# A hybrid attention layer on one core: gates in halves, mixed tiles split earlier, residual tiles loaded in pairs, weight sums in mid-pair

## The chip, the cores and the metric

The kernel runs on one core of a Trainium2 chip. The metric is device time in microseconds (us) of one execution, as the median of the runs shown. The engines that matter are TensorE (PE in the profile, with PEld for its weight loads), VectorE (DVE), ScalarE (ACT), GpSimd (POOL) and SyncE (SP). In this kernel SP issues all DMA transposes and the stores, and POOL issues the loads of weights and of the residual. Each engine works through its own list of instructions in order; an instruction that waits holds all that stand behind it on that engine.

## What is computed

One layer over 1024 tokens of width 1024, with two groups of 8 heads that read the same normalised input, group A with full attention and group B with attention to a neighbourhood on a 16 x 64 grid. Cut to what matters:

```python
h = _rmsnorm(x, norm_gain[l])
proj = h @ w_in[l]                                   # 1024 x 3328
q_a, k_a, v_a, g_a, q_b, k_b, v_b, g_b = jnp.split(proj, split_at, axis=-1)
q_a, k_a = rope(_rmsnorm(q_a, q_norm_a[l])), rope(_rmsnorm(k_a, k_norm_a[l]))
o_a = _gqa_blocked(q_a, k_a, v_a) * jax.nn.silu(g_a)             # softmax over all keys
o_b = _neighbourhood_attn(q_b, k_b, v_b, na_rpb[l]) * jax.nn.silu(g_b)
mixed = jnp.concatenate([o_a, o_b], axis=-1)
x = x + mixed @ w_out[l]
return _rmsnorm(x, final_norm_gain)
```

`rope` stands for the reference's rotation by cosine and sine tables.

## The kernel before

**Precision.** Every matrix product is made from f16 halves: an operand is scaled, rounded to a high half, and the rest is its low half. A product is three matmuls, high x high, high x low and low x high. "Splitting" a tile means making both halves.

**Tokens.** The 1024 tokens are 8 units u of 128. Projections work on pairs of units (`up`, two units), each pair in one bank of PSUM with 2 x 24 matmuls of 128x256, so 48 matmuls a pair and 24 a chain. The pool `ps_p` of PSUM has two such banks; in the profile a bank is named by the pair that took it, `pj`, `kb`, `po`, or `wt` where a weight sum took it first.

**Weights.** The projections come in 17 groups g of 256 columns: 0 to 2 are k, v and q of group A, 3 to 8 q, k, v of group B, 9 and 10 the gates of B, 11 and 12 the gates of A, 13 to 16 the four blocks of w_out. A group's weights are loaded as f32 into one of two buffers `raw` (1 MB, POOL's queue). `prep_a` squares and sums them on ScalarE into `whl` (L287), `prep_b` adds the sum over the partitions with one tiny matmul into a projection bank (the "weight sum", L299), takes it out on VectorE (L300) and raises it to a power on POOL (L301); `prep_c` makes the high half on ScalarE (L306, twice), `prep_d` the low half on VectorE (L313, twice), and then group g+2 is loaded. The bank of the sum is the one that a later pair will use (list `ahead`), so the sum must wait until that bank's former values were taken out, and that pair until L300 has read the sum.

**Stages.** Phase 1 (to about 101 us) normalises x, transposes it and projects groups 0 to 2. Phase 2 (to about 360 us) runs 64 units of full attention (one head and one token unit each), each a step: QK on TensorE, softmax on VectorE and ScalarE, a DMA transpose of the probabilities, and P x V four steps later. Between them, groups 3 to 8 fill TensorE. Phase 3 (to about 573 us) does the same with 64 units of neighbourhood attention, P x V five steps later, filled with the gates 9 to 12 and then with the output projection of token units 0 to 4. The tail does the output projection of units 5 to 7. A step of phase 3 is QK of one unit (L675, L676), 18 matmuls of filling, and P x V of a former unit (L705 to L707). I count steps through both phases: full attention has steps 1 to 64, neighbourhood unit i is step 65 + i.

**Order.** `Flow.at(delay, pos, ...)` puts a piece of work at one of four places of a later step, "pre" (ahead of QK), "mid" (after QK), "post" (ahead of the filling) and "end". TensorE gets its instructions exactly in the order of the program. The order on the other engines is set by a scheduler, within the dependences, when the kernel is built.

**Mixed rows.** When a token unit's attention is gated, `os_a` (ScalarE's squares L731, VectorE L732 and L733, POOL L734), `os_b` (high half L739 on ScalarE, low half L743 on VectorE) and `os_c` (two DMA transposes, L748: the high half into mA, the low half into mB) split its mixed row for the output projection. The two halves live in a buffer `mhl` that units u and u+2 share, so the squares of u+2 wait for both transposes of u. In the kernel before, units 0 to 3 are split by delays after the last gates of A (`SPLIT_DELAY`), units 4 to 6 in fixed units (`SPLIT_AT`).

**Output.** `out_gen` makes 48 matmuls for two (unit, group) jobs, then VectorE adds them to the residual x2 (L779). x is loaded once more for that: x2 of units 0 and 1 into a `raw` buffer early, of units 2 and 3 together with w_out's third block into the old place of hT (`alloc_x2`, L759 and L762), of 4 and 5 after the last weights, of 6 and 7 after units 0 and 1 are stored. In the softmax of phase 3, L683 on VectorE finds the row's maximum mx, L685 on POOL scales it, L686 and L687 on ScalarE take the exponentials, L692 on VectorE makes the low half, and L694 on SP transposes.

Of the kernel before, what the change touches and what calls it, by code (L numbers as in the profile page):

```python
# [16 lines left out]
P = 128  # L17
# [11 lines left out]
SPLIT_AT = (39, 55, 56)  # L29
SPLIT_DELAY = (1, 2, 1, 3)  # L30
# [58 lines left out]
def kernel(ctx: ExitStack, tc: tile.TileContext, x: bass.AP, w: bass.AP, wo: bass.AP,  # L89
# [65 lines left out]
    def load_w(g):  # L155
        if g == 15:
            t = x2["a"] = wraw.tile([P, 2, 1024], F32, tag="raw", name="x2a")
            for u in range(2):
                x2[u] = t[:, u]
                load_x2(u)  # L160
            return
# [146 lines left out]
    def prep_d(g):  # L308
# [7 lines left out]
        if g == 15:  # L316
            load_x2(4)
            load_x2(5)
# [18 lines left out]

    def prep(g):
        if g == 2:
            at(5, "pre", prep_a, g)  # L340
            at(5, "end", prep_b, g)
            at(6, "pre", prep_c, g)
            at(6, "post", prep_d, g)
            at(7, "pre", load_w, g + 2)
            return
# [23 lines left out]
    def chunks(ops, n):  # L369
        for i in range(0, len(ops), n):  # L370
            for o in ops[i:i + n]:
                pe.matmul(*o[0], **o[1])  # L372
            yield

    def proj_pair(g, up, lhs, evac):
# [9 lines left out]
        for i in range(2):  # L385
            ops = [((pt[:, i], lhs(a, k, 2 * up + i), b[:, k]), dict(start=n == 0, stop=n == 23))
                   for n, (k, a, b) in enumerate(seq)]
            yield from chunks(ops, 6)
        evac(pt)
# [123 lines left out]
    def kb_gen(hh, pr, R):  # L513
# [10 lines left out]
        yield from chunks(ops, 3)  # L524
        if R == 0:
            khs[0] = slot("stg", [P, 1024], F16)
        kt = khs[0]
        cs = slice(R * 512, (R + 1) * 512)
        pp = 2 * hh + pr
        at(1, "pre", lambda: act.activation(kt[:, cs], pt, AF.Copy, scale=2.0 ** -14))  # L530
        at(1, "mid", lambda: dve.scalar_tensor_tensor(klo[:, pp, cs], pt, 2.0 ** -14, kt[:, cs],
                                                      op0=OP.mult, op1=OP.subtract))
        if R == 1:
            def cp():
                for e in range(2):
                    for half in range(2):
                        sp.dma_start(khh[half * D:(half + 1) * D, 2 * pp + e], kt[e * D:(e + 1) * D])
            at(1, "post", cp)
# [255 lines left out]
    def fin_b(u):  # L794
# [8 lines left out]
        if u < 2:  # L803
            load_x2(u + 6)
# [236 lines left out]
```

## Time and profile before

| what | value |
|---|---|
| runs (us) | 618.15, 621.88, 621.28 |
| median (us) | 621.28 |
| the profiled execution's own time (us) | 615.87 |
| its span, from the first to the last instruction (us) | 614.1 |
| mean granted clock of TensorE | 0.966 |
| TensorE busy (us, share of the span) | 530.4, 86% |
| VectorE, ScalarE, POOL busy (us) | 435.5, 394.9, 152.6 |

Every duration and wait below comes from that one profiled execution, which is 5.41 us shorter than the median of the runs. A line of a profile names the source line, the engine, the operation, what it writes and reads, and its time; "idle before, releaser" is how long the engine stood still ahead of it and what ended that. The granted clock is the share of full speed at which TensorE was allowed to work. Where the lines of the changed kernel are shown, line numbers are its own and lie some lines lower or higher than those of the kernel before.

### The profile page before, as it was taken

What the parts mean: (1) busy time and instruction counts of PE and PEld (TensorE: products, weight loads), DVE (VectorE), ACT (ScalarE), POOL (GpSimd) and SP (SyncE); (2) the same over time, 40 slices, a digit from 0 to 9 for tenths busy, and PEclk for the clock granted to TensorE, in tenths of its full rate; (3) what the DMA queues carried; (4) which work ended last, traced back from release to release, by engine and by line L of the source; (5) the groups of instructions that cost most, each with busy time, mean ns of one, the idle gap of its engine ahead of it and who ended that gap; (6) DMA issues with size and microseconds to landing.
All of it is one profiled execution on the core that took longest, in us unless ns stands there. A gap on an engine that the chain in (4) does not pass through costs nothing.

```text
span 614.1 us, 13949 instructions
## 1 busy us (share of the span) xinstructions
PE 530.4 (86%) x5541; PEld 405.8 (66%) x5541; DVE 435.5 (71%) x922; ACT 394.9 (64%) x647; POOL 152.6 (25%) x214
## 2 busy tenths in 40 slices
PE   3487989799998999888798989999999767999794
PEld 1375878577774555456676777777777545787683
DVE  4688767977978888777888746565778835877332
ACT  5552645768688688667687646776788957864210
POOL 2386688500000000000000002231324411433100
PEclk9987999999999999999998999999999978999898
DMA  8989543799999999999999974373749979749522
GB/s 231 224 162 234 100 114 95 141 209 197 212 191 186 196 189 196 202 204 172 202 172 183 184 211 119 55 143 65 134 81 151 209 126 177 143 78 199 120 61 69
DMA packets 245971, 97.26 MB, mean 158 GB/s; under 512 B 236561, under 2 KB 237201, under 8 KB 243986
## 3 DMA queue, kind: packets, MB, share of 16 engines
q1 hardware_dynamic: 242306, 75.66, 68.4%
q0 software_dynamic: 3312, 19.92, 11.3%
q10 hardware_dynamic: 288, 0.79, 0.5%
q8 instruction: 43, 0.70, 0.5%
q14 instruction: 22, 0.18, 0.1%
HBM read 31.33 MB, written 4.19 MB: 58 GB/s over the span
## 4 chain that ended last, share of the span: by engine, by line
PE 46%; DMA 23%; DVE 11%; issue 7%; ACT 7%; POOL 4%; SPq 1%; DVEq 0%; POOLq 0%; ACTq 0%
PE pj L372 12%; PE wt L372 10%; DMA ar<-p 9%; PE po L372 7%; DMA mB<-mhl 4%; DMA ar<-ar 3%; PE kb L372 3%; PE s L594 3%; PE s L596 2%; PE sb L676 2%; ACT p L605 2%; ACT p L606 2%; POOL nt L417 2%; DMA pt<-ar 1%; DMA hT<-xhl 1%
## 5 line engine op out<-in xcount | busy, mean ns | idle before, releaser
L372 PEld LDWEIGHTS <-hT 128*128 128x128 f16 x2112 | 207.0, 100 | 76.0 <-issue 19.9
L372 PE MATMUL pj<-whl,hT 128*128 128x256 f16 x1536 | 183.3, 276 | 3.7 <-DMA hT<-xhl 3.7
L372 PE MATMUL wt<-whl,hT 128*128 128x256 f16 x576 | 74.4, 287 | 21.8 <-DVE wss L300 8.9
L603 DVE CUSTOM_DVE_ANT_0 p<-s,sm 128x1024 f32<-128x1024 f32 x64 | 81.9, 1279 | 13.8 <-PE s L596 8.5
L605 ACT ACTIVATE p<-s,nm,sm 128x1024 f16<-128x1024 f32 x43 | 51.8, 1205 | 48.9 <-DMA ar<-p 26.7
L606 ACT ACTIVATE p<-s,nm,sm 128x1024 f32<-128x1024 f32 x64 | 76.9, 1202 | 0.0
L372 PE MATMUL po<-whl,mA 128*128 128x256 f16 x416 | 72.1, 279 | 0.0
L686 ACT ACTIVATE rq<-ar,mx,sm 128x384 f32<-128x384 f32 (+1 forms) x64 | 43.2, 676 | 35.4 <-POOL mx L685 32.9
L611 DVE TENSOR_TENSOR p<-p,p 128x1024 f16<-128x1024 f32 x43 | 52.5, 1221 | 18.4 <-ACT p L606 18.3
L685 POOL TENSOR_SCALAR mx<-mx,sm 128x1 f32<-128x1 f32 x64 | 31.9, 498 | 111.5 <-DVE mx L683 96.9
L372 PE MATMUL po<-whl,mB 128*128 128x256 f16 x208 | 57.9, 278 | 0.0
L301 POOL TENSOR_TENSOR sm<-wss,mh 128x1 f32<-128x1 f32 x17 | 13.4, 789 | 178.2 <-DVE wss L300 177.7
L372 PEld LDWEIGHTS <-mA 128*128 128x128 f16 x512 | 49.3, 100 | 12.3 <-issue 3.9
L594 PE MATMUL s<-kTa,rq 128*128 128x512 f16 x128 | 38.5, 382 | 14.4 <-ACT p L606 14.4
L692 DVE TENSOR_TENSOR ar<-rq,ar 128x384 f16<-128x384 f32 (+1 forms) x64 | 34.2, 536 | 18.0 <-ACT ar L687 17.7
L687 ACT ACTIVATE ar<-ar,mx,sm 128x384 f16<-128x384 f32 (+1 forms) x64 | 42.8, 674 | 1.2
L313 DVE SCALAR_TENSOR_TENSOR whl<-raw,sm,whl 128x1024 f16<-128x1024 f32 (+1 forms) x31 | 41.5, 1348 | 1.3 <-ACT whl L306 1.3
L625 PE MATMUL pv<-va,ar 128*128 128x64 f16 x384 | 38.7, 193 | 3.3 <-DMA ar<-p 2.0
L625 PEld LDWEIGHTS <-ar 128*128 128x128 f16 x384 | 34.5, 98 | 7.2 <-DMA ar<-p 3.3
L627 PE MATMUL pv<-va,ar 128*128 128x64 f16 x384 | 38.7, 193 | 0.0
L626 PE MATMUL pv<-va,ar 128*128 128x64 f16 x384 | 38.7, 193 | 0.0
L306 ACT ACTIVATE whl<-raw,sm 128x1024 f16<-128x1024 f32 x32 | 35.0, 1141 | 3.4 <-POOL sm L301 3.2
(200 smaller groups left out, 1071.7 us busy)
## 6 DMA issues: line engine op xcount, KB each, us to landing
raw<-in_w_dram POOLq DMA_DIRECT2D x11, 1024.0 KB, 6.2
x<-in_x_dram SPq DMA_DIRECT2D x7, 512.0 KB, 6.5
raw<-in_wo_dram POOLq DMA_DIRECT2D x3, 1024.0 KB, 6.1
khh<-ar SPq DMA_DIRECT2D x16, 128.0 KB, 2.9
x2a<-in_x_dram POOLq DMA_DIRECT2D x4, 512.0 KB, 7.6
x2b<-in_x_dram POOLq DMA_DIRECT2D x4, 512.0 KB, 7.9
out_dram<-x2b SPq DMA_DIRECT2D x8, 256.0 KB, 3.6
out_dram<-x2a SPq DMA_DIRECT2D x7, 256.0 KB, 3.1
```

Of the source, the lines that this page charges most:

```text
L313: dve.scalar_tensor_tensor(wp[g][1][:, s], raw[g][:, s], col(S_ + g), wp[g][0][:, s], op0=OP.mult, op1=OP.subtract)
L372: pe.matmul(*o[0], **o[1])
L594: pe.matmul(s[:, c * 512:(c + 1) * 512], q, kTa[:, 4 * c:4 * c + 4, hh], start=True, stop=False)
L603: dve.tensor_tensor_reduce(out=p32, in0=s, in1=col(SHA).to_broadcast([P, 1024]), scale=col(NSA), scalar=3e38, op0=OP.add, op1=OP.min, accu ...
L605: act.activation(hl[:, 0], s, AF.Exp, bias=nm, scale=col(SCA))
L606: act.activation(p32, s, AF.Exp, bias=nm, scale=col(SCA), accum_out=sums[hh, u][:, h:h + 1])
L611: dve.tensor_tensor(hl[:, 1], p32, hl[:, 0], op=OP.subtract)
L625: pe.matmul(o, pt[:, kt], va[:, kt, hh, 0], start=kt == 0, stop=False)
L626: pe.matmul(o, pt[:, kt], va[:, kt, hh, 1], start=False, stop=False)
L627: pe.matmul(o, pt[:, 8 + kt], va[:, kt, hh, 0], start=False, stop=kt == 7)
L686: act.activation(p32, t, AF.Exp, bias=mx, scale=col(SCB + hh), accum_out=sums["b", u][:, h:h + 1])
L687: act.activation(hl[:, 0], t, AF.Exp, bias=mx, scale=col(SCB + hh))
```

## The change

It has four parts.

1. The gates of A are no longer made group by group (group 11 for all four pairs, then group 12) but by halves of the tokens: group 11 for pairs 0 and 1, group 12 for pairs 0 and 1, then both for pairs 2 and 3. The mixed rows of token units 0 to 3 are now split in the fixed units 26, 27, 29 and 31 (plus the five of the skew, which makes 32 to 37), through the same hook as those of 4 to 6. The delays of the weights' preparation stand in the table `PREP`.
2. A weight sum is no longer issued ahead of a step's filling, but at the end of a chain, so in the middle of a pair (`sums_now`, called by `chunks`); it still goes into the bank of the next pair. The high halves, the low halves and the load of g+2 follow one, one and two steps later. What takes a pair's values out is set going in the step of the pair's last matmul and no longer in the call after it.
3. x2 of units 0 and 1 is loaded when the last gates are done, of units 2 and 3 after the first additions to units 0 and 1 (`more_x2`; a copy from x2 of unit 1 on POOL holds the load back until then), of units 4 and 5 after the low halves of group 15, of 6 and 7 after those of group 16. w_out's third block is loaded into the ordinary `raw` buffer.
4. The scaling of mx in the softmax of phase 3 (L685, 64 instructions of 128x1) moves from POOL to VectorE. The words for the change do not name this.

The core of the diff:

```diff
-SPLIT_AT = (39, 55, 56)
-SPLIT_DELAY = (1, 2, 1, 3)
+SPLIT_AT = (26, 27, 29, 31, 39, 55, 56)
+PREP = {2: 4, 3: 0, 4: 2, 12: 0, 13: 0}
...
-        if g == 15:
-            load_x2(4)
-            load_x2(5)
+        if g > 14:
+            t = wraw.tile([P, 2, 1024], F32, tag="raw", name=f"x2{g}")
+            for i in range(2):
+                x2[2 * g - 26 + i] = t[:, i]
+                load_x2(2 * g - 26 + i)
...
     def prep(g):
...
-        d = 0 if g < 4 else 2 if g == 4 else 1
+        d = PREP.get(g, 1)
         at(d + 1, "pre", prep_a, g)
-        at(d + 2, "post", prep_b, g)
-        at(d + 3, "pre", prep_c, g)
-        at(d + 3, "post", prep_d, g)
-        if g + 2 < 17:
-            at(d + 4, "pre", load_w, g + 2)
+        at(d + 2, "mid", pend.append, g)
+
+    def sums_now():
+
+        while pend:
+            g = pend.pop(0)
+            prep_b(g)
+            at(1, "pre", prep_c, g)
+            at(1, "post", prep_d, g)
+            if g + 2 < 17:
+                at(2, "pre", load_w, g + 2)
...
-    def chunks(ops, n):
+    def chunks(ops, n, then=None):
         for i in range(0, len(ops), n):
             for o in ops[i:i + n]:
                 pe.matmul(*o[0], **o[1])
+            if i + n >= len(ops):
+                (then or sums_now)()
...
-        pool.tensor_scalar(mx, mx, col(NSB + hh), LN_P, op0=OP.mult, op1=OP.add)
+        dve.tensor_scalar(mx, mx, col(NSB + hh), LN_P, op0=OP.mult, op1=OP.add)
...
     def alloc_x2():
-        c = one.tile([P, 2, 2, 1024], F32, tag="hT1", name="x2b")
-        raw[15] = c[:, 0].rearrange("p a (b c) -> p (a b) c", c=GC)
-        for u in range(2, NU):
-            x2[u] = x2["a"][:, u - 6] if u > 5 else c[:, int(u < 4), u % 2]
-
+        c = one.tile([P, 4, 1024], F32, tag="hT1", name="x2b")
+        for u in range(4):
+            x2[u] = c[:, u]
+        load_x2(0)
+        load_x2(1)
+
+    def more_x2():
         for u in (2, 3):
-            pool.tensor_copy(x2[u][:, :1], rws[3][:, 3:4])
+            pool.tensor_copy(x2[u][:, :1], x2[1][:, :1])
             load_x2(u)
-        pool.dma_start(raw[15], wo[2])
...
+        def then():
+            at(1, "mid", add)
+            if jobs[-1] == (1, 13):
+                at(1, "post", more_x2)
...
-    fl.add(*group(11, [g_gen(11, up, mixA, slice(0, GC), False) for up in UP]))
-    fl.add(*group(12, [g_gen(12, up, mixA, slice(GC, 512), False) for up in UP]))
+    ga = [[g_gen(GA + i, up, mixA, slice(i * GC, i * GC + GC), False) for up in UP] for i in range(2)]
+    fl.add(*group(11, ga[0][:2]), *ga[1][:2], *ga[0][2:], *group(12, ga[1][2:]))
```

On TensorE the first projection step of the output (units 0 and 1, group 13) begins at step 106 and that of units 2 and 3 at step 109, in both kernels. The weight sum of group 13 stands at step 98 before and at step 105 now, that of group 14 at step 109 before and at step 110 now; the first matmuls with these weights stand at steps 106 and 112. Between a sum and the first matmul with its weights lay 54 matmuls or more for groups 13 and 14, and lie 24 for groups 13 to 16 now, beside QK and P x V.

**SP, the middle of phase 3.** L694 (L692 now) are the softmax transposes, one a step; L748 are the two transposes of a mixed row, of units 0 (mhl_6077), 1 (mhl_6130), 2 (mhl_6224) and 3 (mhl_6304). Before:

```order
132 L694 DMA_TRANSPOSE ar<-ar 128x6x128 x27
133 L748 DMA_TRANSPOSE mA_1058<-mhl_6077 128x8x128
134 L748 DMA_TRANSPOSE mB_4725<-mhl_6077 128x8x128
135 L694 DMA_TRANSPOSE ar<-ar 128x6x128
136 L748 DMA_TRANSPOSE mA_1058<-mhl_6130 128x8x128
137 L748 DMA_TRANSPOSE mB_4725<-mhl_6130 128x8x128
138 L694 DMA_TRANSPOSE ar<-ar 128x6x128 x4
139 L748 DMA_TRANSPOSE mA_1059<-mhl_6224 128x8x128
140 L748 DMA_TRANSPOSE mB_4726<-mhl_6224 128x8x128
141 L694 DMA_TRANSPOSE ar<-ar 128x6x128
142 L748 DMA_TRANSPOSE mA_1059<-mhl_6304 128x8x128
143 L748 DMA_TRANSPOSE mB_4726<-mhl_6304 128x8x128
```

Now, with units 0 (mhl_5986), 1 (mhl_6038), 2 (mhl_6130) and 3 (mhl_6227); eight softmax transposes stand ahead of the first row in both:

```order
132 L692 DMA_TRANSPOSE ar<-ar 128x6x128 x21
133 L748 DMA_TRANSPOSE mA_1072<-mhl_5986 128x8x128
134 L692 DMA_TRANSPOSE ar<-ar 128x6x128
135 L748 DMA_TRANSPOSE mB_4725<-mhl_5986 128x8x128
136 L692 DMA_TRANSPOSE ar<-ar 128x6x128 x2
137 L748 DMA_TRANSPOSE mA_1072<-mhl_6038 128x8x128
138 L748 DMA_TRANSPOSE mB_4725<-mhl_6038 128x8x128
139 L692 DMA_TRANSPOSE ar<-ar 128x6x128
140 L748 DMA_TRANSPOSE mA_1073<-mhl_6130 128x8x128
141 L748 DMA_TRANSPOSE mB_4726<-mhl_6130 128x8x128
142 L692 DMA_TRANSPOSE ar<-ar 128x6x128 x5
143 L748 DMA_TRANSPOSE mA_1073<-mhl_6227 128x8x128
```

Unit 0's first transpose stood behind 35 softmax transposes and now stands behind 29; unit 2's stood behind 40 and now stands behind 32, unit 3's behind 41 and now behind 38.

**ScalarE, at the first output projections.** L731 are the squares of units 4 (mhl_6576, now mhl_6564) and 5 (mhl_7253, now mhl_7257). L306 (L300 now) makes the high halves of the next weights, of group 14 before (whl_6473) and of group 13 now (whl_6210). Before:

```order
361 L287 ACTIVATE whl_6734,wss_6735<-x2b 128x2048
362 L686 ACTIVATE rq,sumb_6346<-ar,mx_2_6431,sm 128x384
363 L731 ACTIVATE mhl_6576,os_6575<-mA_1060 128x512
364 L686 ACTIVATE rq,sumb_6346<-ar,mx_3_6478,sm 128x384
365 L306 ACTIVATE whl_6473<-raw_5702,sm 128x1024 x2
366 L687 ACTIVATE ar<-ar,mx_2_6431,sm 128x384
```

Now:

```order
352 L685 ACTIVATE ar<-ar,mx_7_6300,sm 128x384
353 L731 ACTIVATE mhl_6564,os_6563<-mA_1074 128x512
354 L684 ACTIVATE rq,sumb_6339<-ar,mx_0_6340,sm 128x384
355 L731 ACTIVATE mhl_7257,os_7256<-mA_1074 128x512
356 L300 ACTIVATE whl_6210<-raw_5304,sm 128x1024 x2
357 L685 ACTIVATE ar<-ar,mx_0_6340,sm 128x384
358 L562 ACTIVATE ar<-pj_3_6309,sm 128x512
```

The first squares of unit 5 moved ahead of a weight group's high halves, which were group 14's and are group 13's now.

**POOL and VectorE, at the additions to x.** On POOL, L759 before loaded w_out's third block and L762 x2 of units 2 and 3; L685 is the scaling of mx, L734 belongs to a split. Before:

```order
146 L685 TENSOR_SCALAR mx_1_6387<-mx_1_6387,sm 128x1
147 L759 DMA x2b<-in_wo_dram 128x2048
148 L734 TENSOR_TENSOR os_6303<-os_6303,mh 128x1
149 L685 TENSOR_SCALAR mx_2_6431<-mx_2_6431,sm 128x1
150 L757 COPY x2b<-os_6303 128x1 x2
151 L762 DMA x2b<-in_x_dram 128x1x1024 x2
```

Now, where L763 loads x2 (units 0 and 1 first, then 2 and 3), L159 w_out's third block, and L759 is the copy that holds the second load back:

```order
101 L295 TENSOR_TENSOR sm<-wss_6211,mh 128x1
102 L715 TENSOR_TENSOR mB_4727<-mB_4727,ar 128x256
103 L763 DMA x2b<-in_x_dram 128x1x1024 x2
104 L159 DMA raw_6425<-in_wo_dram 128x2048
105 L759 COPY x2b<-x2b 128x1 x2
106 L763 DMA x2b<-in_x_dram 128x1x1024 x2
```

On VectorE now, L772 is the addition of units 2 and 3, L307 the low halves of group 14 (whl_6469), L681 and L683 belong to a softmax:

```order
739 L690 TENSOR_TENSOR ar<-rq,ar 128x384
740 L740 RECIPROCAL os_6563<-os_6563 128x1
741 L772 SCALAR_TENSOR_TENSOR x2b<-po_13_6524,rw_13_6525,x2b 128x256 x2
742 L307 SCALAR_TENSOR_TENSOR whl_6469<-raw_5702,sm,whl_6469 128x1024
743 L681 ISA ar,mx_7_6658<-sb_4734,bias_4800 128x384
744 L681 ISA mx_7_6658 128x1
745 L307 SCALAR_TENSOR_TENSOR whl_6469<-raw_5702,sm,whl_6469 128x1024
746 L683 TENSOR_SCALAR mx_7_6658<-mx_7_6658,sm 128x1
```

Before, the low halves of group 14 (L313) stood ahead of that addition (L779):

```order
683 L313 SCALAR_TENSOR_TENSOR whl_6473<-raw_5702,sm,whl_6473 128x1024 x2
684 L683 ISA ar,mx_6_6619<-sb_4733,bias_4800 128x384
685 L683 ISA mx_6_6619 128x1
686 L692 TENSOR_TENSOR ar<-rq,ar 128x384 x2
687 L732 TENSOR_TENSOR os_6575<-os_6575 128x1
688 L779 SCALAR_TENSOR_TENSOR x2b<-wt_6522,rw_13_6532,x2b 128x256 x2
```

The load of x2 for units 2 and 3 moved behind w_out's third block and behind the additions of units 0 and 1, and the addition of units 2 and 3 moved ahead of group 14's low halves.

More of the change, by code (lines that the diff above doesn't have):

```diff
@@ L569, in mul @@
                 dve.scalar_tensor_tensor(m, th, col(G2 + g - GB), m, op0=OP.mult, op1=OP.mult)
+                ready.add(("a", up, cols.start))
             at(1, "mid", mul)
[L571 to L575 removed]
             if g == GA + 1 and up == 3:
@@ L726, in os_a @@
     def os_a(u):
+        assert all({("b", u, c), ("a", u // 2, c * GC)} <= ready for c in range(2))
         t = rws[u] = tn(f"os{u}", 4, "os")
```

79 lines of the change are left out of this document (31 added, 48 removed).

## The prediction

> **What bounds the kernel now.** I read the page of the profile first, then TensorE's waits, then the chain of waits, then the stretches of the span in which the chain leaves TensorE, and last the timelines of the queues there. The page:
>
> ```profile
> span 614.1 us, 13949 instructions
> PE 530.4 (86%) x5541; PEld 405.8 (66%) x5541; DVE 435.5 (71%) x922; ACT 394.9 (64%) x647; POOL 152.6 (25%) x214
> ```
>
> TensorE is busy for 530.4 of 614.1 us, so what can be won without less work are its 84 us of idle time and the time it runs at a lower clock. The change removes no matmul. Its worth is therefore a list of TensorE's waits that go and waits that come. TensorE's waits (us in total, how often, the longest):
>
> ```profile
> PE s L594 <- ACT p L606: 14.4, 12, 1.9
> PE wt L372 <- DVE wss L300: 13.5, 10, 2.5
> PE wt L372 <- DMA mB<-mhl: 7.0, 1, 7.0
> PE sb L705 <- DMA ar<-ar: 5.5, 2, 4.4
> PE pvb L705 <- DMA ar<-ar: 2.6, 1, 2.6
> PE wt L299 <- DVE x2a L779: 0.9, 1, 0.9
> PE wt L299 <- DVE ar L568: 0.6, 1, 0.6
> PE wt L299 <- DVE mB L565: 0.5, 1, 0.5
> ```
>
> Rows 2 and 6 to 8 are the weight sums (L299, and L300 behind it): 13.5 + 0.9 + 0.6 + 0.5 = 15.5 us. Row 3 is the out-projection waiting for the low half of unit 2's mixed rows. Rows 4 and 5 are neighbourhood attention waiting for softmax transposes. The chain (start, duration, what) shows where these lie:
>
> ```profile
> 442.66 2.07 PE pj L372 x18
> 445.42 2.07 PE pj L372 x18
> ...
> 470.04 5.32 DMA mB<-mhl
> ...
> 483.41 12.75 DMA mB<-mhl
> ...
> 532.50 0.75 DVE x2a L779 x2
> ...
> 573.04 23.99 PE po L372 x208
> ```
>
> An undisturbed step of phase 3 takes 445.42 - 442.66 = 2.76 us, a matmul 23.99 / 208 = 0.115. From 483 to 496 us the program waits for one transpose of 12.75 us, where that of unit 0 had taken 5.32. Three timelines (SP, POOL, ACT) show what lay beside it and what stood behind it:
>
> ```profile
> 483.41 4.20 SPq L748 DMA_TRANSPOSE mB<-mhl  x1
> 481.83 0.64 POOL L759 DMA_DIRECT2D x2b<-in_wo_dram  x1
> 484.12 1.13 POOL L762 DMA_DIRECT2D x2b<-in_x_dram  x2 [0.17 <-POOL x2b L757]
> 496.18 0.63 ACT L731 ACTIVATE mhl<-mA 128x512 bf16<-128x512 f32 x1 [5.53 <-DMA mB<-mhl]
> 497.50 2.17 ACT L306 ACTIVATE whl<-raw,sm 128x1024 f16<-128x1024 f32 x2
> ```
>
> One 1 MB and two 512 KB loads were issued within 3.4 us around it, and ScalarE stood 5.53 us at the squares of unit 4 (they share unit 2's buffer), with the scaling of the next weights behind. The stretches after such waits (length, busy us of PE, PEld, DVE, ACT, POOL, then clock, DMA share, GB/s):
>
> ```profile
> 492.00:495.00 3.00, 0.00 (x0) 0.00 (x0) 0.00 (x0) 0.00 (x0) 0.00 (x0) 0.50 1.39 146
> 495.00:498.00 3.00, 1.71 (x9) 1.21 (x10) 0.00 (x0) 1.82 (x5) 0.00 (x0) 0.50 1.25 225
> 498.00:501.00 3.00, 3.00 (x23) 1.94 (x22) 1.54 (x6) 3.00 (x5) 0.99 (x2) 0.59 0.37 74
> 510.00:513.00 3.00, 2.64 (x19) 1.58 (x20) 1.83 (x6) 2.97 (x6) 0.92 (x2) 0.62 1.54 186
> 513.00:516.00 3.00, 3.00 (x28) 2.20 (x27) 1.58 (x5) 1.25 (x3) 0.33 (x1) 0.81 0.86 174
> 121.00:124.00 3.00, 2.69 (x14) 1.96 (x14) 2.66 (x13) 3.00 (x7) 1.47 (x1) 0.60 1.03 194
> 124.00:127.00 3.00, 3.00 (x40) 2.30 (x38) 2.32 (x2) 1.94 (x2) 0.00 (x0) 0.83 1.10 126
> 92.00:95.00 3.00, 3.00 (x30) 2.70 (x28) 1.65 (x5) 1.29 (x2) 3.00 (x5) 1.00 0.27 50
> ```
>
> After the 7.0 and 2.6 us waits, and after one of 2.48 us that ends at 121, the granted clock is 0.50 to 0.62 for a slice; after one of 2.04 us that ends at 91 it stays at 1.00. TensorE's busy time times what the clock lacks is 1.7 x 0.50 + 3 x 0.41 = 2.1 us after the first, 2.64 x 0.38 + 3 x 0.19 = 1.6 after the second, 2.69 x 0.40 + 3 x 0.17 = 1.6 after the third. I price a wait of over 2.4 us at its length and 1.8 us more.
>
> **Removed.** (1) Unit 2's transpose: with the gates of A in halves unit 2 is transposed behind 32 softmax transposes instead of 40, eight steps or 22 us earlier for the same place of use, and the two x tiles and wo's third block leave the burst at 482. Its cover is these 22 us, more than the worst 12.75. 7.0 + 2.1 = 9.1 us. (2) The transpose wait at 510 (2.6 + 1.6 = 4.2) and the two at 567 and 573 (5.5 + 1.8 = 7.3), if the softmax transposes no longer queue behind split transposes and x loads: 11.5. (3) and (4) The sums. Single waits of theirs (the last number; the third kind comes four times, the first and the last shown):
>
> ```profile
> 91.31 0.49 PE L372 MATMUL wt<-whl,hT 128*128 128x256 f16 x3 [2.04 <-DVE wss L300]
> 121.31 0.56 PE L372 MATMUL wt<-whl,hT 128*128 128x256 f16 x3 [2.48 <-DVE wss L300]
> 151.25 0.49 PE L372 MATMUL wt<-whl,hT 128*128 128x256 f16 x3 [1.45 <-DVE wss L300]
> 284.88 0.49 PE L372 MATMUL wt<-whl,hT 128*128 128x256 f16 x3 [1.45 <-DVE wss L300]
> ```
>
> (3) Phase 3 has what is left of 13.5 without these: 13.5 - 2.0 - 2.5 - 4 x 1.45 = 3.2 us, and the three evacuation waits of 0.9, 0.6 and 0.5: 5.2. With (1) and (2) phase 3 loses 9.1 + 11.5 + 5.2 = 25.8 us.
> (4) Phase 2 has the 2.48 us with its clock, 4.1 us, and four of 1.45: 5.8, together 9.9. These four do not turn into time one for one: in phase 2 the next bound is close by, as the 14.4 us in twelve waits for ScalarE's L606 show, and this stretch of 15 us:
>
> ```profile
> 300.00:315.00 15.00, 13.10 (x177) 10.47 (x176) 11.90 (x20) 10.71 (x15) 0.00 (x0) 1.00 1.01 180
> ```
>
> The DMA engines' share is 1.01 there, and TensorE idles for 1.9 of 15 us with no sum near. I take the early 4.1 and a fifth of the 5.8: 5.3 us, with 0 and 9.9 as ends.
>
> **Added.** The sum now comes 24 matmuls ahead of the first use of its weights (groups 13 to 16), where those of 13 and 14 had 54. What must happen in between, in the sums of before (group 13):
>
> ```profile
> 456.99 0.15 DVE L300 TENSOR_SCALAR wss<-wt 128x1 f32<-128x1 f32 x1
> 458.67 2.17 ACT L306 ACTIVATE whl<-raw,sm 128x1024 f16<-128x1024 f32 x2
> 459.88 2.48 DVE L313 SCALAR_TENSOR_TENSOR whl<-raw,sm,whl 128x1024 f16<-128x1024 f32 x2
> ```
>
> From L300 to the end of the first low half (459.88 + 1.24) are 4.1 us, and the sum itself lies some 0.5 before: 4.6. 24 matmuls are 24 x 0.115 = 2.8 us, and the QK and PV of a step 2.76 - 2.07 = 0.7: 3.5 or, with two such, 4.2. So a bare wait of 0.4 to 1.1 us, four times, and at two places more. The first sum that moves so is group 2's, in phase 1: no QK or PV beside it, 4.6 - 2.8 = 1.8 us of wait in the place of the 2.04 that ended at 91, 1.8 more if the clock falls. Ends -2.0 (hidden) and +2.3 (as the 2.48 us wait, with its clock): I take +1, the clock being nearer to falling there than not.
> S1, group 13. The low half stands behind ScalarE's hi, and this now stands behind the squares of unit 5 (L731), which wait until both transposes of unit 3 have landed. The row for such a place is the 5.53 us wait above; a transpose like unit 0's (5.32) frees it sooner than that of 12.75. I take 3, about the middle between 0.4 and 5.53, 1.4 for the evacuation that the sum itself now meets (the 0.9 and 0.5 rows together), and the clock's 1.8: 6.2. Ends 2 and 13 (the 12.75 us transpose again).
> S2, group 14. On VectorE the low halves of whl14 come behind the additions of units 2 and 3 to x; x of these units is loaded only after units 0 and 1 were added, because a copy on POOL waits for that, and behind wo's third block in the same queue.
>
> ```profile
> raw<-in_wo_dram POOLq DMA_DIRECT2D x3, 1024.0 KB, 6.1
> x2b<-in_x_dram POOLq DMA_DIRECT2D x4, 512.0 KB, 7.9
> ```
>
> The additions of units 0 and 1 stand in the middle of step 110, whl14 is wanted in step 112; with steps of 2.76 us some 5 us lie between. Issue costs 1.3 (484.12's row), the landing 7.9, two additions 0.75 (L779's row), the low half 1.2: 11.2. Late by 6.2; if x had landed, by 0.75 + 1.2 less QK and PV, 1.2, since the additions need the pair that ends just before. I take a landing some 2.5 us shorter, since no burst of 2 MB lies ahead, so 3.7, and the clock's 1.8: 5.5. Ends 1.2 and 12 (a landing of 12 us). Behind VectorE there wait the softmaxes of the following units, whose P x V is five steps off.
> S3 and S4, groups 15 and 16: 1.4 (there additions part the two low halves) and the bare 0.7, with 0 and 4 as ends. Tail: the last softmax transposes now alternate with those of unit 6: 2.5, nearly half of the 5.5 in row 4 (0 to 6).
> New waits: 6.2 + 5.5 + 1.4 + 0.7 + 2.5 = 16.3.
> mx on VectorE:
>
> ```profile
> L685 POOL TENSOR_SCALAR mx<-mx,sm 128x1 f32<-128x1 f32 x64 | 31.9, 498 | 111.5 <-DVE mx L683 96.9
> ```
>
> 64 x 0.15 (L300's row, same form) = 9.6 us go to VectorE, which is idle for 29% of the span; each softmax loses a hop of 0.5 us. Five steps of skew hide both: 0. Were VectorE the late one (S2's place), its 0.15 us a step would cost 2 us at most. The early split's transposes and x loads (4 MB as before, in pairs) cost nothing where they lie on gates; that cover is five steps of P x V ahead.
>
> **Sum.** -25.8 + 16.3 = -9.5 in phase 3, -5.3 in phase 2, +1 in phase 1: -13.8. The profiled run took 615.87 us (span 614.1), 5.41 below the median 621.28 of the runs shown; 621.28 - 13.8 = 607.5, and I say 607.
>
> [...] The 2.48 and 2.6 us waits above were followed by a clock of 0.6. [...] The landing of x was 7.9 us above. [...]
>
> **Rivals.** (a) The wait only moves: the squares of unit 5 hold ScalarE as those of unit 4 did, for the 12.75 us transpose. S1 becomes 13 and S2, pushed with the rest, 8: -13.8 + 6.8 + 2.5 = -4.5, 617, and the four 1.45s may give nothing, 618. For it speaks that the buffers are shared as before; against it, that no 2 MB burst lies beside unit 3's transposes any more.
> (b) Slower: VectorE is held at the addition of units 2 and 3. If wo's block (6.1 us) stands ahead in the queue and x takes as long as the 12.75 us transpose, these add 6.1 + 4.9 = 11 to S2, and the softmaxes behind it let TensorE wait for P x V a second time, as 4.4 + 2.6 us did, with two falls of the clock: 11 + 7 + 3.6 = 21.6 more than forecast, +7.8, 629; with S1 at its end 636. It decides, alone, from a landing of some 20 us on (S2 20 instead of 5.5). Against it: 1 + 1 MB at 200 GB/s are 10 us.
> (c) All sums turn into time and S1 and S2 hide: -25.8 + 7 - 9.9 = -28.7, or -24 with half of phase 2's: 592.5 to 597.
>
> **Chances.** Forecast 0.58 (598 to 615), (a) 0.18, (b) 0.13, (c) 0.11. Within 1% is 615.1 to 627.5, about what a measurement here can tell from no change. Faster: 0.58 + 0.11 and a fifth of (a), 0.72; within: the rest of (a) and a part of (b), 0.17; slower 0.11. The range 596 to 620 leaves out (b) and most of (c), 0.2.
>
> **What would show it.** Right: no TensorE wait on mB<-mhl; L300 gone from the waits but at group 13 or 14; a wait of 3 to 5 us for whl13 with ScalarE's L731 idle before on mB<-mhl, and one for whl14 with VectorE's addition idle on an x load; the four 1.45 us waits gone but TensorE's waits on L606 grown. Wrong: waits on ar<-ar as long as before, or S2 above 12 us.

## The result, and the profile after

The changed kernel takes 610.2 us in the median of 4 runs (607.6 to 614.18), the kernel before 621.3 (618.15 to 621.88): the ratio is 0.9866, 95% interval 0.9821 to 0.9911. The ratio goes by the fast runs and is not quite the quotient of the two medians, which is 0.982. Run again later beside the experiments the changed kernel took 610.03 where the kernel before took 616.79: 0.9891 (0.9848 to 0.9934). So it is faster by 1.1 to 1.3% by the ratios, some 7 to 11 us by the medians. The predicted 607 lay in the right direction and 3 us too low; against 621.28 it was a ratio of 0.977, below the interval.

The profiled execution took 611.81 us. Its page and TensorE's waits:

```profile
span 610.0 us, 13863 instructions
PE 534.4 (88%) x5541; PEld 405.4 (66%) x5541; DVE 440.6 (72%) x986; ACT 394.9 (65%) x647; POOL 119.3 (20%) x150
```

```profile
PE s L592 <- ACT p L604: 14.6, 13, 1.7
PE wt L369 <- ACT whl L300: 9.2, 4, 6.1
PE wt L369 <- DVE whl L307: 7.6, 6, 2.4
PE pv L623 <- DMA ar<-p: 7.4, 4, 2.5
...
PE sb L703 <- DMA ar<-ar: 4.3, 3, 2.0
PE wt L293 <- DVE sum L630: 3.0, 1, 3.0
...
PE wt L293 <- DVE rq L552: 2.3, 1, 2.3
```

The wait on mB<-mhl is gone, and so are the waits for the weight sum itself (L300 before, 13.5 us). In their place stand waits for the weights' halves (L300 and L307 are now the high and the low half), two waits of a sum for its bank (L293, 3.0 and 2.3 us), and P x V of full attention waits 7.4 us for its transposes, where it had waited 2.0. (Of the 9.2 us for the high halves one wait of 6.1 ends at 32.5 us; there the kernel before had waited 6.8.) The row of before for P x V:

```profile
PE pv L625 <- DMA ar<-p: 2.0, 4, 0.7
```

Cut at the first QK of steps 1, 68, 104 and 128, the two profiled executions compare like this (us):

| stretch | before | after | difference | predicted |
|---|---|---|---|---|
| to step 1 (phase 1) | 101.8 | 101.0 | -0.8 | +1 |
| steps 1 to 68 (phase 2 and its end) | 268.4 | 273.1 | +4.6 | -5.3 |
| steps 68 to 104 | 101.7 | 99.2 | -2.5 | |
| steps 104 to 128 | 83.0 | 80.0 | -3.0 | |
| step 128 to the end | 59.2 | 56.8 | -2.5 | |
| steps 68 to the end | 243.9 | 236.0 | -7.9 | -9.5 |

Phase 3 and the tail gained what was forecast, less 1.6 us. Phase 2 went the other way. In phase 1 the difference of 0.8 us shows nothing: over the profiles of all kernels below this stretch lies between 99.7 and 102.1 us.

The two places where new waits were forecast, on ScalarE and on VectorE (start, duration, idle before):

```profile
481.40 0.63 ACT L731 ACTIVATE mhl<-mA 128x512 bf16<-128x512 f32 x1 [0.67 <-DMA mB<-mhl]
481.94 0.19 ACT L731 ACTIVATION_READ_ACCUMULATOR mhl<-mA 128x1 f32 x1
482.03 2.17 ACT L300 ACTIVATE whl<-raw,sm 128x1024 f16<-128x1024 f32 x2
```

```profile
483.20 2.48 DVE L307 SCALAR_TENSOR_TENSOR whl<-raw,sm,whl 128x1024 f16<-128x1024 f32 x2 [1.74 <-ACT whl L300]
...
502.06 0.48 DVE L772 SCALAR_TENSOR_TENSOR x2b<-po,rw,x2b 128x256 f32<-128x256 f32 x1 [1.00 <-DMA x2b<-in_x_dram]
502.46 1.27 DVE L307 SCALAR_TENSOR_TENSOR whl<-raw,sm,whl 128x1024 f16<-128x1024 f32 x1
```

Both mechanisms are there: unit 5's squares wait for unit 3's transposes with the high half behind them, and the addition to x waits for its load with a low half behind it. But unit 3's transposes had no load beside them and were quick, as the chain shows (with the load of x2 that the second place waits for):

```profile
478.03 3.35 DMA mB<-mhl
...
495.59 6.45 DMA x2b<-in_x_dram
```

### The profile page after: what moved, and what is told of

It is laid out like the page before. It is cut to its first block, busy times and chain, and to the rows that moved or that the text cites. A ratio compares the mean times of both kernels' runs of the same rounds, so it can differ in the third digit from the quotient of the medians.

```text
span 610.0 us, 13863 instructions
## 1 busy us (share of the span) xinstructions
PE 534.4 (88%) x5541; PEld 405.4 (66%) x5541; DVE 440.6 (72%) x986; ACT 394.9 (65%) x647; POOL 119.3 (20%) x150
## 4 chain that ended last, share of the span: by engine, by line
PE 44%; DMA 14%; issue 14%; DVE 13%; POOL 6%; ACT 5%; SPq 1%; DVEq 0%; POOLq 0%; ACTq 0%
PE pj L369 14%; PE wt L369 7%; DMA ar<-p 6%; PE po L369 5%; PE kb L369 4%; DMA ar<-ar 4%; PE s L592 3%; PE s L594 2%; POOL nt L417 2%; PE sb L674 2%; DVE whl L307 2%; ACT p L604 2%; DVE p L601 1%; PE sb L673 1%; ACT p L603 1%
## 5 line engine op out<-in xcount | busy, mean ns | idle before, releaser
L369 PE MATMUL pj<-whl,hT 128*128 128x256 f16 x1584 | 189.2, 275 | 3.4 <-DMA hT<-xhl 1.8
L369 PE MATMUL wt<-whl,hT 128*128 128x256 f16 x528 | 68.0, 286 | 14.9 <-ACT whl L300 7.1
L369 PE MATMUL po<-whl,mA 128*128 128x256 f16 x384 | 65.8, 277 | 0.0
L295 POOL TENSOR_TENSOR sm<-wss,mh 128x1 f32<-128x1 f32 x17 | 11.0, 645 | 250.1 <-DVE wss L294 237.4
L369 PE MATMUL po<-whl,mB 128*128 128x256 f16 x192 | 53.1, 277 | 0.0
L592 PE MATMUL s<-kTa,rq 128*128 128x512 f16 x128 | 39.5, 391 | 14.6 <-ACT p L604 14.6
L623 PE MATMUL pv<-va,ar 128*128 128x64 f16 x384 | 39.3, 194 | 8.7 <-DMA ar<-p 7.4
L307 DVE SCALAR_TENSOR_TENSOR whl<-raw,sm,whl 128x1024 f16<-128x1024 f32 (+1 forms) x33 | 44.8, 1371 | 1.9 <-ACT whl L300 1.9
L685 ACT ACTIVATE ar<-ar,mx,sm 128x384 f16<-128x384 f32 (+1 forms) x64 | 42.9, 674 | 1.1
L300 ACT ACTIVATE whl<-raw,sm 128x1024 f16<-128x1024 f32 x34 | 37.1, 1138 | 5.0 <-POOL sm L295 4.9
L681 DVE CUSTOM_DVE_ANT_0 ar<-sb,bias 128x384 f32<-128x384 f32 x48 | 26.6, 555 | 18.4 <-PE sb L674 15.4
L625 PE MATMUL pv<-va,ar 128*128 128x64 f16 x384 | 39.3, 194 | 0.0
L624 PE MATMUL pv<-va,ar 128*128 128x64 f16 x384 | 39.3, 194 | 0.0
```

Source lines behind the costliest of these rows:

```text
L307: dve.scalar_tensor_tensor(wp[g][1][:, s], raw[g][:, s], col(S_ + g), wp[g][0][:, s], op0=OP.mult, op1=OP.subtract)
L592: pe.matmul(s[:, c * 512:(c + 1) * 512], q, kTa[:, 4 * c:4 * c + 4, hh], start=True, stop=False)
L623: pe.matmul(o, pt[:, kt], va[:, kt, hh, 0], start=kt == 0, stop=False)
L624: pe.matmul(o, pt[:, kt], va[:, kt, hh, 1], start=False, stop=False)
L625: pe.matmul(o, pt[:, 8 + kt], va[:, kt, hh, 0], start=False, stop=kt == 7)
L685: act.activation(hl[:, 0], t, AF.Exp, bias=mx, scale=col(SCB + hh))
```

## The experiments

Each ratio is to the kernel before, run beside it on the same chip. The first four ask which part carries the gain.

**Old sums in the changed kernel** (sums_old), the `at(...)` lines of `prep` as before; what takes a pair's values out is set going after the pair again, as before, so this takes back the whole of part 2:

```diff
-        at(d + 2, "mid", pend.append, g)
+        at(d + 2, "post", prep_b, g)
+        at(d + 3, "pre", prep_c, g)
+        at(d + 3, "post", prep_d, g)
```

> The changed kernel with the weight sums (and the taking out of a pair's values) placed as before; gates, splits, x2 and mx as changed. Theory A (the moved sums brought nothing in phase 2: in the changed kernel's trace the waits on L300 are gone there, but two waits of a sum for its bank and four of P x V for transposes have come, and phase 2 is 4.7 us longer than before): within 2 us of the changed kernel's 610.2, so 608 to 612, and in its trace the stretch from step 1 to step 68 is shorter by 3 to 5 us than the changed kernel's 273.1. Rival A' (the sums brought the 5.3 us of the prediction, and the profiled execution of the changed kernel only drew a long phase 2): 614 to 617, and the stretch is not shorter.

614.43 us, ratio 0.9963 (0.9924 to 1.0002): nearly all the gain is gone. The time is in the range of A' (614 to 617), yet steps 1 to 68 took 268.6 us, as theory A had it. The loss is in phase 3: TensorE waited once for 9.34 us. The timeline there (SP, POOL, PE), the transpose for which that wait was (from the chain), and what this kernel's row transposes took to land:

```profile
475.43 1.23 SPq L745 DMA_TRANSPOSE mA<-mhl  x1
476.75 2.95 SPq L745 DMA_TRANSPOSE mB<-mhl  x1
473.92 0.62 POOL L159 DMA_DIRECT2D raw<-in_wo_dram  x1 [4.26 <-DVE whl L307]
476.89 1.05 POOL L760 DMA_DIRECT2D x2b<-in_x_dram  x2 [2.36 <-PE wt L368]
493.16 0.23 PE L700 MATMUL sb<-ar 128*128 128x64 f16 x1 [9.34 <-DMA ar<-ar]
```

```profile
479.87 13.25 DMA ar<-ar
```

```profile
DMA to landing us min/median/max: 3.1/3.6/14.3
```

w_out's third block is loaded when group 13's low half has freed its buffer. With the old sums that was at 473.92, in the changed kernel at 485.97. So the moved sum put off a load, and without it the load and x2's met unit 3's transposes, one of which took 14.3 us, and the softmax transpose behind them, which took 13.25 us. It was this second one for which TensorE waited. This gave theory C, below.

**Moved sums alone** (sums_only), part 2 of the change put into the kernel before:

```diff
-        at(d + 2, "post", prep_b, g)
+        at(d + 2, "mid", pend.append, g)
...
-    def chunks(ops, n):
+    def chunks(ops, n, then=None):
```

> The kernel before with the moved weight sums alone; gates, splits, x2 and mx as before. Theory A: 618 to 622, with at most the 3 us of phase 3's sums gained, and a stretch from step 1 to step 68 as long as the changed kernel's 273.1 us or near it (before: 268.4). Rival A': 613 to 616, with that stretch at 268 or less.

623.36 us, ratio 1.0111 (1.0054 to 1.0168): slower, more than theory A had it. Steps 1 to 68 took 272.8 us, as theory A had it, and TensorE waited 9.79 us for a row's transpose, the slowest of which took 15.1 us:

```profile
504.76 0.39 PE L373 MATMUL po<-whl,mA 128*128 128x256 f16 x1 [9.79 <-DMA mA<-mhl]
```

**Late split** (split_old), the gates group by group, units 0 to 3 by delays, and groups 12 and 13 prepared one step later:

```diff
-SPLIT_AT = (26, 27, 29, 31, 39, 55, 56)
-PREP = {2: 4, 3: 0, 4: 2, 12: 0, 13: 0}
+SPLIT_AT = (39, 55, 56)
+SPLIT_DELAY = (1, 2, 1, 3)
+PREP = {2: 4, 3: 0, 4: 2}
...
-    fl.add(*group(11, ga[0][:2]), *ga[1][:2], *ga[0][2:], *group(12, ga[1][2:]))
+    fl.add(*group(11, ga[0]), *group(12, ga[1]))
```

> The changed kernel with the gates of A group by group and units 0 to 3 split by the old delays; sums, x2 and mx as changed. Theory B (the 12.75 us transpose was late because the 2 MB burst of loads lay beside it, and the change cured it by loading x2 in pairs): within 3 us of the changed kernel, 609 to 613, no TensorE wait on mB<-mhl over 2 us. Rival B' (it was late because it came late, and the earlier split cured it): the 7 us wait and its clock are back, 617 to 620.

623.22 us, ratio 1.0111 (1.0057 to 1.0164). Theory B falls: without the early split all the gain is lost and more, although x2 comes in pairs. Rival B' has the direction, but the time lies above its 617 to 620 too, and its single wait of 7 us is not there. Here the pair of x2 loads (483.56) met unit 2's transposes (483.64 and 484.99), and the slowest took 10.7 us. TensorE waited 0.64 and 3.87 us for the rows and then 5.25 us for VectorE, which had stood 8.44 us for a softmax transpose. The third block of w_out was loaded at another time too (465.92, in the changed kernel 485.97), so this run does not show what the split alone is worth.

**x2 as before** (x2_old):

```diff
+        if g == 15:
+            t = x2["a"] = wraw.tile([P, 2, 1024], F32, tag="raw", name="x2a")
...
-            if jobs[-1] == (1, 13):
-                at(1, "post", more_x2)
```

> The changed kernel with the residual's loads as before (units 2 and 3 with w_out's third block in one burst after the last gates); gates, splits, sums and mx as changed. Theory B: the burst meets the transposes of units 3 and the softmaxes: ScalarE held at the squares of unit 5 for 5 us or more, 615 to 620. Rival B': transposes of units 0 to 2 are done before the burst, and the wait of whl14 behind the addition of units 2 and 3 (2.4 us and 1.7 of clock) goes: 606 to 611.

608.29 us, ratio 0.9861 (0.9806 to 0.9915), the same as the changed kernel, so rival B' holds. The pairs of x2 are worth nothing by themselves; the burst did no harm to the rows because it came at 478.11, when unit 3's transposes, issued at 473.88 and 475.24, had landed or were about to (the second at 478.62; none took over 5.4 us). Softmax transposes did meet it, and the slowest landed after 13.64 us, but no wait of TensorE for one ends between 478 and 560 us. What did come was one of 2.62 us for a weight sum, whose bank the addition to x left late because its x2 load took 12.73 us.

**Loads held back** (gate_loads), theory C's own test, the kernel with the old sums and this:

```diff
+        if g == 15:
+            pool.tensor_copy(raw[g][:, 0, :1], mT[3][1][:, 0, :1])
         pool.dma_start(raw[g], w[g] if g < 13 else wo[g - 13])
...
+        for u in range(2):
+            pool.tensor_copy(x2[u][:, :1], mT[3][1][:, 0, :1])
+            load_x2(u)
```

> The kernel with old weight sums and new gates, splits, x2 and mx (sums_old), with one thing more: the loads of w_out's third block and of x2 of units 0 and 1 are held back until unit 3's rows are transposed (a one-element copy on POOL reads the transposed row first). Theory C (a row's two transposes take 12 to 14 us when loads from POOL's queue are issued while they are in flight, and 3 to 5 us otherwise; what moved the time in phase 3 is whether they meet): unit 3's low transpose lands within 6 us instead of 14.3, the 9.34 us wait of P x V at 493 goes with its clock, 605 to 609. Rival C' (it is the amount of data in the stretch that counts, not the meeting): the loads, some 4 us later, make another wait of the same size, 612 to 616.

606.56 us, ratio 0.9836 (0.9797 to 0.9876) where the same kernel without the gate had 0.9963 (0.9924 to 1.0002). Its timeline (SP and POOL), and the landing of its row transposes:

```profile
476.39 1.23 SPq L747 DMA_TRANSPOSE mA<-mhl  x1
477.71 1.29 SPq L747 DMA_TRANSPOSE mB<-mhl  x1
481.31 0.46 POOL L160 CAST raw<-mB 128x1 f32<-128x1 f16 x1 [1.93 <-DMA mB<-mhl]
482.07 0.63 POOL L161 DMA_DIRECT2D raw<-in_wo_dram  x1
482.69 1.08 POOL L763 DMA_DIRECT2D x2b<-in_x_dram  x2
```

```profile
DMA to landing us min/median/max: 3.1/3.3/5.1
```

The same loads, moved by 8 and 6 us to behind the transposes, leave none over 5.1 us. Theory C holds, and rival C' falls: the same amount of data was loaded. P x V still waited once for a softmax transpose, 3.73 us, so the loads are not free.

**Loads held back in the kernel before** (before_gate):

```diff
-            pool.tensor_copy(x2[u][:, :1], rws[3][:, 3:4])
+            pool.tensor_copy(x2[u][:, :1], mT[3][1][:, 0, :1])
             load_x2(u)
+        pool.tensor_copy(raw[15][:, 0, :1], mT[3][1][:, 0, :1])
         pool.dma_start(raw[15], wo[2])
...
-        pool.tensor_scalar(mx, mx, col(NSB + hh), LN_P, op0=OP.mult, op1=OP.add)
+        dve.tensor_scalar(mx, mx, col(NSB + hh), LN_P, op0=OP.mult, op1=OP.add)
```

> The kernel before with two edits: the loads of w_out's third block and of x2 of units 2 and 3 are held back until unit 3's rows are transposed, and the scaling of mx stands on VectorE (so that POOL, when it waits, holds no softmax). Gates, splits and sums as before. Theory C (the 12.75 us transpose was slow because loads were issued while it was in flight): unit 2's low transpose lands within 6 us, the 7.0 us wait and its clock go, 606 to 611 where the kernel before takes 617, 0.98 to 0.99 of it. Rival B' (the late split itself was the cost): TensorE still waits for unit 2's or 3's rows for 5 us or more, 614 to 618.

611.54 us, ratio 0.9919 (0.9887 to 0.9951): the gain is just short of what theory C gave (606 to 611, 0.98 to 0.99). Landing of the row transposes, and TensorE's longest wait of phase 3:

```profile
DMA to landing us min/median/max: 3.1/4.1/5.3
```

```profile
506.24 0.23 PE L705 MATMUL pvb<-rq,ar 128*128 128x64 f16 x1 [5.73 <-DMA ar<-ar]
```

The slow transpose is cured, with the split as late as before. Theory C holds here too, and B' falls: TensorE's longest wait for a row was 0.84 us. But the loads, now at 492 to 497, met softmax transposes, and P x V waited 5.7 us for one. Part of the wait only moved, to 5.73 us where 7.01 and 2.62 had been. That an earlier split leaves room for the loads as well fits this, but no run tests it alone.

**Old sums up to group 11** (hyb with x2_old's loads, hyb_after with the changed kernel's; in phases 1 and 2 what takes a pair's values out is set going after the pair again):

```diff
+        if g < 12:
+            at(d + 2, "post", prep_b, g)
+            at(d + 3, "pre", prep_c, g)
+            at(d + 3, "post", prep_d, g)
+            at(d + 4, "pre", load_w, g + 2)
+            return
```

> The kernel with x2 as before (x2_old), whose weight sums up to group 11 stand as before and from group 12 on in mid-pair, so that phase 2 is that of the kernel before. Theory A (moved sums cost phase 2 some 3 us: 269 to 273 from step 1 to step 68 with them, 268.4 and 268.6 without): 2 to 4 us under x2_old, 604 to 607, stretch 268 to 269. Rival A'': the difference in phase 2 is chance from execution to execution: the same as x2_old, 607 to 610.

606.38 us, ratio 0.985 (0.9806 to 0.9894).

> The changed kernel with the weight sums up to group 11 as before and from group 12 on in mid-pair. Theory A: 2 to 4 us under the changed kernel, 605 to 608 on a chip where the kernel before takes 617 to 621. Rival A'': the same as the changed kernel, 608 to 611.

607.7 us, ratio 0.9845 (0.9798 to 0.9893). By the ratios both lie under their partners (0.9861 for x2_old, 0.9866 and 0.9891 for the changed kernel), by 1 to 3 us, which the intervals do not separate. The stretch from step 1 to 68 was 269.3 and 267.1 us. Over all profiles of this study it is 267.1 to 270.4 us with the old sums in phase 2 (seven executions, mean 268.4) and 269.1 to 273.1 with the moved ones (seven, mean 271.1): 2.7 us more, with a small overlap. Theory A holds on average. These runs move the sums together with the moment at which a pair's values are taken out, so they do not say which of the two it is.

**Unit 3's split later** (split_u3_35):

```diff
-SPLIT_AT = (26, 27, 29, 31, 39, 55, 56)
+SPLIT_AT = (26, 27, 29, 35, 39, 55, 56)
```

> The changed kernel with unit 3's split set for unit 35 instead of 31; on ScalarE this puts the high halves of group 13 ahead of the first squares of unit 5, and leaves SP's order as it is. Theory D (S1 of the prediction: the wait for group 13's weights was ScalarE held at unit 5's squares): the wait at step 106 falls from 3.3 us to 1.5 or less, 2 to 3 us under the changed kernel. Rival D' (the wait is the bare length of the chain from sum to low half against 24 matmuls): it stays at 2.5 us or more, within 1.5 us of the changed kernel.

610.63 us, ratio 0.9896 (0.9855 to 0.9938), not to be told from the changed kernel. The wait for group 13's weights fell from 3.3 us (0.39, 1.86 and 1.05) to 1.9:

```profile
479.57 0.27 PE L369 MATMUL wt<-whl,mA 128*128 128x256 f16 x1 [0.86 <-ACT whl L300]
480.89 0.27 PE L369 MATMUL wt<-whl,mA 128*128 128x256 f16 x1 [1.05 <-DVE whl L307]
```

That is between D and D', and the time is as D' had it. 1.4 us went with this edit: 1.0 of the wait for the high half, which now stands ahead of unit 5's squares, and the 0.39 us that the sum had waited for its bank. 1.9 us stayed, the bare length of the chain.

**mx back on POOL** (mx_pool):

```diff
-        dve.tensor_scalar(mx, mx, col(NSB + hh), LN_P, op0=OP.mult, op1=OP.add)
+        pool.tensor_scalar(mx, mx, col(NSB + hh), LN_P, op0=OP.mult, op1=OP.add)
```

> The changed kernel with the scaling of mx on POOL as before. Theory E (the prediction: hidden by the skew of five steps, worth nothing): within 1.5 us of the changed kernel run beside it. Rival E' (the shorter softmax chain and the free POOL queue, whose waiting loads no longer hold a softmax, are part of the gain): 3 us slower or more.

609.97 us, ratio 0.9898 (0.9865 to 0.9932), beside the changed kernel's 0.9891. Theory E holds.

**The changed kernel again** (after_again), unchanged:

> The changed kernel once more, beside the others on the same chip. Theory A (its phase 2 is longer by 3 us than with the old sums, in every execution): the stretch from step 1 to step 68 at 269 to 273 us again; ratio to the kernel before 0.983 to 0.990. Rival A'': the stretch falls to 268 or less.

610.03 us, ratio 0.9891 (0.9848 to 0.9934); steps 1 to 68 took 272.3 us, as theory A had it.

**A better one** (best), hyb_after with unit 3's split at 35:

```diff
-SPLIT_AT = (26, 27, 29, 31, 39, 55, 56)
+SPLIT_AT = (26, 27, 29, 35, 39, 55, 56)
...
+        if g < 12:
+            at(d + 2, "post", prep_b, g)
```

> The changed kernel with the weight sums up to group 11 as before (hyb_after) and unit 3's split set for unit 35. Theory A and D together: phase 2 3.0 us shorter and group 13's wait 1.4 us shorter than in the changed kernel run beside it, so 3 to 5 us under it. Rival: these waits are filled by others, within 1.5 us of it.

603.98 us, ratio 0.9805 (0.9771 to 0.984): 6 us under the changed kernel beside it, whose interval begins at 0.9848, and so a little more than the 3 to 5 expected. It beats both kernels. In its profile steps 1 to 68 took 267.9 us, and phase 3 with the tail 234.4, the shortest such end of all profiles. Alone, the two edits had brought 1 to 3 us (hyb_after) and nothing to be seen (split_u3_35); why they bring 6 together is not shown.

## Why the prediction was right, and where it was wrong

**Right: the direction, and phase 3.** Step (1), unit 2's transpose, is gone with its clock, as is the wait at 510 in step (2). The new waits were forecast at 16.3 us; with the clock priced in the same way they are about 16 (15.7), so what was removed came to 7.9 + 15.7 = 23.6 of the 25.8:

| term | predicted | measured | from |
|---|---|---|---|
| S1 | 6.2 | 4.6 | 0.39 + 1.86 + 1.05 us of wait, 1.3 of clock |
| S2 | 5.5 | 4.1 | 2.42 us, and 1.7 of clock |
| S3 | 1.4 | 1.0 | 0.98 us |
| S4 | 0.7 | 1.7 | 1.69 us |
| tail | 2.5 | 3.2 | 1.20 + 2.00 us |
| not forecast | | 1.1 | P x V at 531.74 us for a softmax transpose |

The clock's part is worked out from these slices of the changed kernel (PE's busy time times what the clock lacks):

```profile
483.00:486.00 3.00, 1.73 (x14) 1.25 (x14) 2.80 (x3) 3.00 (x5) 0.03 (x1) 0.70 0.91 207
486.00:489.00 3.00, 3.00 (x23) 1.99 (x21) 2.10 (x6) 2.97 (x6) 0.53 (x1) 0.73 1.05 243
...
504.00:507.00 3.00, 3.00 (x26) 2.37 (x24) 3.00 (x7) 1.45 (x4) 0.63 (x1) 0.62 0.03 5
507.00:510.00 3.00, 3.00 (x27) 2.06 (x25) 1.64 (x7) 0.83 (x3) 0.00 (x0) 0.82 0.95 270
```

Rival (a) did not come, since unit 3's transposes landed quickly. Rival (b)'s mechanism did, and was worth 1.00 us of VectorE's time: x2 landed in 6.45 us on the chain, nearer to my 5.4 than to the median of before. mx was worth nothing, as forecast. Phase 1 (+1): the 2.04 us at 91 is gone, and group 2's halves are waited for 0.99, 1.14 and 0.33 us at 78 to 81, about the 1.8 expected, at a clock of 1.00.

**Wrong: step (4), phase 2.** I counted the waits on L300 as gone and let a fifth of the four late ones turn into time: -5.3 us. They are gone, and phase 2 is longer, by 4.6 us in the two executions compared and by 2.7 in the mean of all. The step had looked only at what the pair waits for and not at what the sum itself waits for. In mid-pair the sum comes 24 matmuls after the pair that held its bank, and VectorE has not always taken that pair's values out yet. The rows of the changed kernel at 123 us:

```profile
121.20 1.22 DVE L609 TENSOR_TENSOR p<-p,p 128x1024 f16<-128x1024 f32 x1
122.34 0.17 DVE L629 RECIPROCAL sum<-sum 128x4 f32<-128x4 f32 x1
122.42 0.85 DVE L502 SCALAR_TENSOR_TENSOR ar<-pj,ar 128x128 f16<-128x128 f32 x4
```

```profile
123.42 0.16 PE L293 MATMUL wt<-wss,mh 128*128 128x1 bf16 x1 [2.99 <-DVE sum L630]
```

L502 reads the bank (pj) and stands behind two softmaxes' work; the sum starts 0.15 us after it. (The row names L630, which ran in between.) I had charged such an evacuation 1.4 us at S1 and nothing in phase 2, though VectorE is busier there (80% of steps 1 to 68 of before, 71% of its whole span). The same wait came at 123 and at 290 to 294 us in all seven profiles with moved sums and in none of the others.
It does not account for all. TensorE's waits of over 0.25 us between 105 and 372 us are 28.2 us before and 28.5 after: what the sums no longer wait (8.8) is waited by sums for banks (5.3) and by P x V for transposes (8.6, before 5.2). So no waiting was saved, and nearly all of the added time is the clock's. The stretch from step 1 to step 68, before:

```profile
101.78:370.21 268.43, 240.50 (x2827) 172.04 (x2824) 214.79 (x357) 195.87 (x265) 22.57 (x24) 0.99 0.99 188
```

after:

```profile
100.95:374.02 273.07, 244.45 (x2826) 172.93 (x2824) 212.35 (x361) 195.46 (x262) 19.04 (x22) 0.97 0.98 187
```

The same matmuls take 4 us more of TensorE's time, at a clock of 0.97 instead of 0.99. Slice by slice (3 us each) the clock falls in two places before, from 120 and from 330 us (to 0.67 and 0.50), and in four after, from 216, 264, 291 and 333 (to 0.50, 0.64, 0.59 and 0.67). TensorE's busy time times what the clock lacks there is 3.0 us before and 7.0 after. The three places that are new lie behind P x V's waits of 2.47 and 1.52 us, each followed by one of QK for ScalarE, and behind the sum's 2.28 us. The first of them:

```profile
217.32 0.20 PE L623 MATMUL pv<-va,ar 128*128 128x64 f16 x1 [2.47 <-DMA ar<-p]
```

```profile
216.00:219.00 3.00, 0.95 (x24) 0.85 (x25) 0.00 (x0) 1.64 (x2) 0.00 (x0) 0.83 1.11 229
219.00:222.00 3.00, 2.20 (x6) 0.82 (x6) 1.52 (x2) 3.00 (x5) 0.00 (x0) 0.50 0.89 173
```

So the four removed waits of 1.45 us had cost no clock (it was 1.00 in the slices in which they end and in the next ones), and those that took their place did. Over all profiles this loss is 2.9 to 6.0 us with the old sums and 5.9 to 9.1 with the moved ones; the 6.0 are before_gate's, so an execution can lose as much without moved sums. That the sums' waits would be taken over by others was in the text ("the next bound is close by"); that the exchange could cost was bounded away by "0 and 9.9 as ends". The lower end should have gone below zero. The bound that I had named did not take them over: TensorE's waits for ScalarE's L606 went from 14.4 us to 14.6 only. That the longer waits of P x V come with part 2 of the change is shown by their coming and going with it (3.8 to 6.3 us without it, 6.7 to 8.9 with it); by which path, stays open.

**Half right: step (1)'s reason.** I gave two reasons for the slow transpose to go, the earlier split and the broken burst. To break the burst is not needed (x2_old), and an early split with it is not enough (sums_old, 614.43). What decides is what POOL loads while a row's transposes fly. In four kernels x2's loads met those of unit 2 or 3, and one took 10.7 (split_old) or, with w_out's block ahead, 12.7 to 15.1 us (before, sums_old, sums_only). Not every meeting is that dear: in ten kernels unit 4's transposes met w_out's last block, 1 MB, and landed in 4.6 to 8.7 us. Moving the loads switched the slow transpose off in two kernels, in before_gate together with mx, which mx_pool shows to be worth nothing in the changed kernel. So the changed kernel owes its moved sums a part of its gain because they put off one load by 12 us; in phase 2 the same edit costs. The slowest row transpose took 14.3 us in sums_old, where POOL's loads were in flight beside it, and 5.1 in gate_loads, where they were held back; by which mechanism a load slows it, no run shows.

**The base, and luck.** The sum was made on one execution of 615.87 us and then set against the median of 621.28. Beside the three later groups of runs the kernel before took 616.8 to 617.3 us in the median. Against its own base the sum said 602; the changed kernel's profile shows 611.81 and its runs 610. Most of the 8 us between are phase 2's, with 5.3 us not gained and 2.7 lost. That 607 came within 3 us of the result is therefore in part luck: a base some 4 us too high made up for half of what phase 2 did not bring.

## What to carry to other kernels

When a small step is moved into the middle of a stream, list what it waits for itself at the new place, not only what no longer waits for it; and if its end frees a buffer, ask which load now starts when, and what is in flight then. A DMA transpose on which engines wait is best kept apart from bulk loads by an explicit dependence (here the slowest row transpose went from 14.3 us in sums_old to 5.1 in gate_loads), and moved early enough that the loads behind it do not meet the next ones. A wait that goes where another bound is close can come back as several smaller ones and as a lower clock (here 0.97 for 0.99 over steps 1 to 68), so its term's range reaches below zero.

## What the runs showed of the hardware

The clock did not follow the length of a wait as I had priced it ("over 2.4 us"). After the 2.99 us wait that ends at 123.42 it stays full; after the 2.28 us wait that ends at 292.43 it falls to 0.59 in the next slice:

```profile
121.00:124.00 3.00, 0.58 (x17) 0.58 (x18) 2.79 (x11) 2.70 (x5) 0.14 (x1) 1.00 1.11 212
124.00:127.00 3.00, 3.00 (x36) 2.34 (x33) 2.51 (x6) 1.58 (x2) 1.38 (x1) 1.00 1.14 97
...
291.00:294.00 3.00, 1.57 (x23) 1.45 (x24) 3.00 (x7) 0.06 (x1) 0.00 (x0) 0.84 1.05 198
294.00:297.00 3.00, 3.00 (x24) 1.78 (x22) 1.77 (x4) 3.00 (x4) 0.56 (x1) 0.59 0.64 131
```

So the length of the wait alone does not decide: one of 2.99 us left the clock at 1.00, while those of 2.28 us here and of 2.48 and 2.62 in the kernel before were followed by 0.59, 0.60 and 0.62. What decides, no run shows.
Of the row transposes (128 x 1024 halves) of all 14 profiles whose landing is in the trace, the 144 with none of POOL's loads in flight beside them landed in 3.1 to 5.3 us, and the 40 with some in 3.3 to 15.1: up to 8.7 us beside one block of w_out (1 MB), up to 10.7 (split_old) beside loads of x2, and up to 12.7 to 15.1 us (before 12.7, sums_old 14.3, sums_only 15.1) where block and pair came together (2 MB).
